# Up's first four blocks: four products in turn for all, weight sums made in DRAM, and the output factors in another pool

## The chip, the cores and the metric

The kernel runs on one core of a Trainium2 chip. The metric is device time in microseconds (us) of one execution. Three runs of the kernel before are shown, and one further execution was profiled.

The engines go by the profile's names: PE multiplies matrices (PEld is its weight load), DVE works elementwise, ACT applies functions and copies, POOL here fills memory and issues transfers, SP issues transfers. An engine takes its instructions in one fixed order.

## The reference

One decoder block on 512 rows of 2048 channels, in float32:

```
z = rms_norm(x, norm1_g) @ w_in                       # input projection
o_rw, o_att = rwkv7_mix(z...), swa_attention(z...)    # two mixers
x = x + (g_rw * (o_rw @ w_branch[:RW]) + g_att * (o_att @ w_branch[RW:])) @ w_out
u = rms_norm(x, norm2_g) @ w_up                       # 2048 -> 2 * 5632, "Up"
c = causal_conv3(u) ; val, gate = split(c, 2)
x = x + (silu(gate) * val) @ w_down                   # "Down"
```

## The kernel before

**Stages.** Input projection with both mixers; branch products; output product (`w_out`); Up with convolution and gate; Down. Every float32 operand of a large product is split into a high part (ACT, a copy to the rounded format `F32R`) and a low part (DVE, the difference), and a product is three matmuls: high-high, high-low, low-high.

**Products of halves.** Output product, Up and Down cut both operands into 2 x 2 halves and run seven products of halves in place of eight, with sums and differences of the halves (Strassen's scheme in Winograd's form).

For the output product and Down, the sums of weights are made in DRAM while the input projection runs. `jobs` (L216) lists them, 120 in all: 32 for `o`, 88 for `dn`. `sums_along` (L224) takes the next: SP copies a piece of 512 KB in DRAM, POOL adds a second piece by an accumulating transfer. `load_w` (L233), the loader of the projection's and the branch stage's weights, calls it at every third load (`wp["step"]`, L167), later at every fourth and twelfth; Up calls it for the jobs left (L1194).

**Up.** 44 blocks `f`, each a `Block` (L1043): 128 channels of `val` and `gate`, contracted over two halves of 1024, for two halves of the 512 rows. The left factors of the seven products are weights, the right factors (`bq`) are made once from the normalised rows:

| product | weights | right factor | sums into |
|---|---|---|---|
| P1 | a11 = w[0,0] | b11 | X |
| P2 | a12 = w[0,1] | b21 | Z |
| P7 | s3 = w[0,0] + w[1,0] | t3 | Y |
| P6 | a11 + s1 | t2 | X |
| P5 | s1 = w[1,0] + w[1,1] | t1 | X |
| Q4 | a22 = w[1,1] | t4 | Y |
| P3 | a11 + s1 + a12 | b22 | X |

`load` (L1050) lets SP fetch a tile of 512 KB; for s3 and s1, POOL then adds the second weight by an accumulating transfer. `sums` (L1058) makes the left factors of P6 and P3 on DVE (L1063). `parts` (L1065) splits a left factor: ACT makes `whi` (L1069), DVE `wlo` (L1070), in three buffers each. `mm` (L1073) issues 24 matmuls (L1087). `out` (L1090) copies X to `u` on ACT (L1103) and adds Y or Z on DVE (L1105, L1107). X and Z of blocks 0 to 3 share one PSUM bank. `u` has two buffers, for even and odd blocks. `conv` (L1109) is the convolution and gate of a block in five parts, seven for odd blocks.

**Order.** `pin` (L203) is `keep_in_program_order`: pinned instructions of an engine keep the order of the program. What isn't pinned is placed by the framework's planner, by priority and readiness.

`steps` (L1140) lists the products: for blocks 0 to 3 (`NPRE`) P1 four times, P2 four times, P7 four times, then the other four products in pairs of blocks; from block 4 on, block by block. `run(i)` (L1186) first splits the weights of step i + 2 (`prep`, L1174), then issues the matmuls and outputs of step i. `prep` also issues the next loads and takes one part of a convolution, two in a stretch. Loads go into a ring of six tiles `raw` and one of two tiles `a11`, and a load waits until the tile's earlier user is done. Of blocks 0 to 3, w[0,0] and w[0,1] are loaded twice (`p11`, `p12`, then `a11`, `a12`).

**From output product to Up.** In the last of the output product's seven rounds (L1205 to L1224), `normalise` scales the first half of the rows, `transposed` (L1009) turns q11 and q21 by PE, and `split_q` (L1032) splits them to b11 and b21, 2048 elements a row. `taken_out` (L957) adds the last round's product to x (L968), and `row_done` squares it. The second half of the rows is scaled by the transposing matmul itself, with `diagonals` (L1001) as its right side. The calls from L1237 to L1279 interleave the first twelve steps with the transposes of q12 and q22 and with the differences and splits of the other five right factors. These, in the version before, are not pinned.

**Output factors.** `fetch` (L929) loads a pair of the output product's right factors from DRAM into the pool `hp` (L864): three buffers on the right side of memory, opened ahead of the branch stage.

Of the kernel before, what the change touches and what calls it, by code (L numbers as in the profile page):

```python
# [134 lines left out]
def block_kernel(ctx: ExitStack, tc: tile.TileContext, d: Dims, a: dict, out: bass.AP):  # L135
# [79 lines left out]

    jobs = []  # L216
    for w in ("o", "dn"):
        for kinds in (
            (("s1", (1, 0), (1, 1)), ("s3", (0, 0), (1, 0))),
            (("s2", "s1", (0, 0)),),  # L220
            (("s4", "s2", (0, 1)),),
        ):
            jobs += [(w, k, c, q) for c in range(NB[w]) for q in range(2) for k in kinds]
    def sums_along():  # L224

        if not jobs:
            return lambda: None
        w, (n, first, second), c, q = jobs.pop(0)
        dst = sum_d[w][n][c][q]
        pin(sync.dma_start(dst, quarter(w, first, c)[q], max_dma_last_dim=4096))  # L230
        return lambda: pool.dma_start(dst, quarter(w, second, c)[q], accum_op=ALU.add, max_dma_last_dim=4096)

    def load_w(src):  # L233
        nk, ncol = src.shape[1:]
        n = nk * ncol
        raw = wp["raw"].tile([P, 512], F32, name="raw", tag="raw")[:, :n].rearrange("p (k c) -> p k c", c=ncol)
        wp["last"] = sync.dma_start(raw, src)
# [3 lines left out]
        dve.tensor_tensor(lo, raw, hi.bitcast(F32), op=ALU.subtract)  # L241
        wp["n"] += 1
        if wp["n"] % wp["step"] == 0:
            sums_along()()
        return hi, lo
# [763 lines left out]
    def transposed(tps, i, q, dg=None):  # L1009
# [11 lines left out]
        for k in range(KH):  # L1021
            src, g = pss[k // 2][:, k % 2], col("n2g", i * KH + k)
            dst = q[:, 2 * k // KH, k % (KH // 2) * TH : (k % (KH // 2) + 1) * TH]
            if k % 2:
                dve.tensor_scalar(dst, src, g, None, op0=ALU.mult)
            else:
                act.activation(dst, src, AF.Copy, scale=g)

    def halves(t):
        return t.rearrange("p (a k) s -> p a (k s)", a=2)  # L1030

    def split_q(n, q):  # L1032
        hi, lo = (halves(x) for x in bq[n])
        act.activation(hi, q, AF.Copy)
        dve.tensor_tensor(lo, q, hi.bitcast(F32), op=ALU.subtract)

    us = []
    dve.tensor_scalar(cw[:, 0:3, NF:], cw[:, 0:3, NF:], -1.0, None, op0=ALU.mult)


    NPRE = 4

    class Block:  # L1043
# [3 lines left out]
        def __init__(self, f):  # L1047
            self.f, self.w, self.hl = f, {}, {}

        def load(self, n):  # L1050
            f, w = self.f, self.w
            at = {"p11": (0, 0), "p12": (0, 1), "a11": (0, 0), "a12": (0, 1), "s3": (0, 0), "s1": (1, 0), "a22": (1, 1)}
            w[n] = raw_tile("a11", 2) if n in ("a11", "p11") else raw_tile()
            sync.dma_start(w[n], a["w_up"][(f, *at[n])])
            if n in ("s3", "s1"):
                pool.dma_start(w[n], a["w_up"][f, 1, int(n == "s1")], accum_op=ALU.add)

        def sums(self, n):  # L1058

            w = self.w  # L1060
            if n in ("P6", "P3"):
                t = w["a11"]
                pin(dve.tensor_tensor(t, t, w["s1" if n == "P6" else "a12"], op=ALU.add))  # L1063

        def parts(self, n):  # L1065
            one = "ap"[self.f < NPRE]
            t = self.w[{"P1": one + "11", "P2": one + "12", "P7": "s3", "P6": "a11", "P5": "s1", "Q4": "a22", "P3": "a11"}[n]]
            hi, lo = (hlp.tile([P, WC], F32R, name=f"w{e}", tag=f"w{e}") for e in ("hi", "lo"))
# [4 lines left out]
        def mm(self, n):  # L1073
# [4 lines left out]
            if n == "P7":  # L1078
                self.Y = upy.tile([P, S], F32, name="Y", tag="Y")[:, :TH]
            ps = getattr(self, {"P2": "Z", "P7": "Y", "Q4": "Y"}.get(n, "X"))  # L1080
            start = n in ("P1", "P7") or n == "P2" and self.f >= NPRE
            whi, wlo = (x.rearrange("p (k c) -> p k c", c=P) for x in self.hl.pop(n))
# [7 lines left out]
        def out(self, n):  # L1090
# [3 lines left out]
            if n == "P1" and self.f < NPRE:  # L1094
                self.t1 = up.tile([P, TH], F32, name="t1", tag="t1", bufs=NPRE)
                pin(act.activation(self.t1, X, AF.Copy))
                return

            i, j, ps, first = {"P1": (0, 0, X, True), "P2": (0, 0, Z, False), "P6": (1, 0, X, True), "P5": (1, 1, X, True),
                               "Q4": (1, 0, Y, False), "P3": (0, 1, X, True)}[n]  # L1100
# [5 lines left out]
            else:  # L1106
                pin(dve.tensor_tensor(u, self.t1 if n == "P2" and self.f < NPRE else u, ps, op=ALU.add))  # L1107

# [40 lines left out]
    queue, order = [], {x: i for i, x in enumerate(steps)}  # L1149
    loads = [(f + e, n) for f in range(0, NPRE, 2) for n in ("p11", "p12") for e in range(2)] + [(f, "s3") for f in pre]  # L1150
    for f in range(NF):
        loads += [(f, n) for n in ("a11", "s3", "s1", "a12", "a22") if n != "s3" or f >= NPRE]
    held = {True: [], False: []}
    for f, n in loads:
        kind = n in ("p11", "a11")
        users = {"p11": ("P1",), "p12": ("P2",), "s3": ("P7",), "s1": ("P5", "P6"), "a22": ("Q4",)}.get(n, ("P3",))
        ring, deep = held[kind], 2 if kind else 6
# [28 lines left out]
    def run(i):  # L1186
        f, n = steps[i]
        prep(i + 2, 2 if 3 * NPRE <= i < 7 * NPRE else 1)
        B[f].mm(n)
        if n != "P2" or f >= NPRE:  # L1190
            B[f].out(n)
        if n == "P3":
# [8 lines left out]
    with tc.tile_pool(name="sqp", bufs=1, side="right", reuse_waits="tile") as sqp:  # L1201
# [3 lines left out]
        for i in range(len(PRODUCTS)):  # L1205
# [6 lines left out]
            for c in range(NB["o"]):  # L1212
                steps_of("o", i, acc[nm], c, hp)
                if last and c == NB["o"] - 4:
                    transposed(tps, 0, q11)
                    split_q("b11", q11)
                if last and c == NB["o"] - 3:
                    transposed(tps, 1, q21)
                    split_q("b21", q21)
            if last:  # L1220
# [24 lines left out]
    tpx.close()  # L1245
    run(4)
    dve.tensor_tensor(q12, q22, q12, op=ALU.subtract)
    split_q("t3", q12)
    tcx.close()
    x1q.close()  # L1250
    run(5)
    run(6)
    split_q("t1", q11)
    run(7)
    upy = psx.enter_context(tc.tile_pool(name="uppy", bufs=4, space=PSUM, side="right", reuse_waits="tile"))
    run(8)
    dve.scalar_tensor_tensor(q11, q11, -1.0, q22, op0=ALU.mult, op1=ALU.subtract)
    split_q("t2", q11)
    run(9)
    run(10)  # L1260
    split_q("b22", q22)
    run(11)
    dve.scalar_tensor_tensor(q21, q11, -1.0, q21, op0=ALU.mult, op1=ALU.subtract)
    split_q("t4", q21)
    x1s.close()
    upu = upx.enter_context(tc.tile_pool(name="upu", bufs=1, side="left", reuse_waits="tile"))
    for i in range(2):
        u = upu.tile([P, 2, S + 2], F32, name=f"u{i}")
        pool.memset(u[:, :, 0:2], 0.0)
        us.append(u)  # L1270
    upcx = ExitStack()
    upc = upcx.enter_context(tc.tile_pool(name="upc", bufs=1, side="right", reuse_waits="tile"))
    hp0 = upcx.enter_context(tc.tile_pool(name="hhl0", bufs=1, side="right", reuse_waits="tile"))
    for f in range(2):
        B[f].out("P2")
    for i in range(3 * NPRE, len(steps)):
        run(i)
        if steps[i] in ((2, "P6"), (2, "Q4")):
            B[2 + (steps[i][1] == "Q4")].out("P2")  # L1279
        if steps[i] == (NF - 2, "P7"):  # L1280
# [105 lines left out]
```

## Time and profile before

| | us |
|---|---|
| median of 3 runs | 2830.01 (2829.44 to 2835.7) |
| the profiled execution | 2830.7 |
| its span in the profile | 2828.9 |
| PE busy | 2774.4 |
| DVE busy | 1987.5 |
| ACT busy | 1342.1 |
| POOL busy | 225.1 |

The granted clock of the profiled execution is 0.996 on average. An engine's busy time is the union of its instructions; matmuls overlap each other, so a matmul lasts longer in the profile than the distance from one to the next. A row of the waits gives who waited for whom, the total in us, how often, and the longest. A row of the chain gives start, length and what ran; "x24" is the number of instructions merged. A row of the groups gives line, engine and operation, output and inputs with their shape, count, then busy time and mean ns of one, then the idle time ahead of them. In the profile's names, X stands for the bank of X and Z, `x` for the rows of x and the halves q, `b` and `t` for right factors, `raw` and `a` for weight tiles, `c` for the tiles of the convolution, and `dg` for the diagonals.

### The profile page before, as it was taken

What the parts mean: (1) busy time and instruction counts of PE and PEld (TensorE: products, weight loads), DVE (VectorE), ACT (ScalarE), POOL (GpSimd) and SP (SyncE); (2) the same over time, 40 slices, a digit from 0 to 9 for tenths busy, and PEclk for the clock granted to TensorE, in tenths of its full rate; (3) what the DMA queues carried; (4) which work ended last, traced back from release to release, by engine and by line L of the source; (5) the groups of instructions that cost most, each with busy time, mean ns of one, the idle gap of its engine ahead of it and who ended that gap; (6) DMA issues with size and microseconds to landing.
All of it is one profiled execution on the core that took longest, in us unless ns stands there. A gap on an engine that the chain in (4) does not pass through costs nothing.

```text
span 2828.9 us, 45923 instructions
## 1 busy us (share of the span) xinstructions
PE 2774.4 (98%) x17450; PEld 2403.0 (85%) x17450; DVE 1987.5 (70%) x3437; ACT 1342.1 (47%) x2256; POOL 225.1 (8%) x299
## 2 busy tenths in 40 slices
PE   7999999999999999999999899999999999999999
PEld 5777777777777777888888899999999999888887
DVE  4588677777777774545678777878787878655555
ACT  4355445444544553322465455555545555444444
POOL 0001000000000001011010011011101110000000
PEclk9999999999999999999999999999999999999999
DMA  7865766666666667878777789888988897877775
GB/s 216 227 159 163 187 167 168 175 164 158 175 162 171 160 165 223 234 248 292 237 251 211 210 235 241 229 229 227 241 236 222 228 242 228 315 245 241 256 256 190
DMA packets 223726, 607.04 MB, mean 215 GB/s; under 512 B 24448, under 2 KB 44560, under 8 KB 222480
## 3 DMA queue, kind: packets, MB, share of 16 engines
q1 hardware_dynamic: 156096, 432.64, 47.1%
q0 software_dynamic: 36064, 132.14, 24.5%
q10 hardware_dynamic: 31344, 39.31, 4.0%
q8 instruction: 137, 2.24, 0.3%
q14 instruction: 85, 0.70, 0.1%
HBM read 554.38 MB, written 174.40 MB: 258 GB/s over the span
## 4 chain that ended last, share of the span: by engine, by line
PE 87%; DVE 5%; ACT 3%; DMA 2%; issue 1%; SPq 0%; POOL 0%; ACTq 0%; DVEq 0%; POOLq 0%
PE X L1087 18%; PE X L954 11%; PE acc L256 9%; PE acc L255 9%; PE acc L257 9%; PE Y L954 9%; PE Y L1087 9%; PE Z L1087 4%; DVE wlo L241 1%; PE psS L740 1%; PE psG L731 1%; PE bulk L623 1%; PE bulk L673 1%; PE bulk L534 1%; ACT whi L240 1%
## 5 line engine op out<-in xcount | busy, mean ns | idle before, releaser
L255 PE MATMUL acc<-xhi,whi 128*128 128x512 f32 x1152 | 462.9, 402 | 1.9 <-DVE xlo L301 1.9
L257 PE MATMUL acc<-xhi,wlo 128*128 128x512 f32 x1152 | 463.8, 403 | 0.0
L256 PE MATMUL acc<-xlo,whi 128*128 128x512 f32 x1152 | 462.2, 401 | 0.0
L947 DVE TENSOR_TENSOR wlo<-raw,whi 128x1024 fp32r<-128x1024 f32 x210 | 256.9, 1224 | 205.1 <-ACT whi L946 204.9
L240 ACT ACTIVATE whi<-raw 128x512 fp32r<-128x512 f32 x352 | 220.0, 630 | 375.7 <-PE acc L256 295.1
L946 ACT ACTIVATE whi<-raw 128x1024 fp32r<-128x1024 f32 x210 | 222.8, 1061 | 290.6 <-PE X L954 152.9
L241 DVE TENSOR_TENSOR wlo<-raw,whi 128x512 fp32r<-128x512 f32 x352 | 241.3, 689 | 167.1 <-ACT whi L240 146.9
L1087 PE MATMUL X<-b,whi 128*128 128x256 f32 x1472 | 270.2, 284 | 2.3 <-DVE u L1107 0.9
L1087 PE MATMUL X<-t,whi 128*128 128x256 f32 x1408 | 259.6, 285 | 10.3 <-DVE u L1107 9.8
L1070 DVE TENSOR_TENSOR wlo<-raw,whi 128x1024 fp32r<-128x1024 f32 x176 | 215.0, 1222 | 77.6 <-ACT whi L1069 77.3
L1087 PE MATMUL Y<-t,whi 128*128 128x256 f32 x1408 | 257.1, 283 | 0.0
L255 PEld LDWEIGHTS acc<-xhi,whi 128*128 128x128 f32 x1152 | 217.6, 189 | 43.4 <-issue 2.5
L256 PEld LDWEIGHTS acc<-xlo,whi 128*128 128x128 f32 x1152 | 217.5, 189 | 41.9 <-issue 3.3
L257 PEld LDWEIGHTS acc<-xhi,wlo 128*128 128x128 f32 x1152 | 217.5, 189 | 38.3 <-issue 1.1
L1069 ACT ACTIVATE whi<-a 128x1024 fp32r<-128x1024 f32 x132 | 139.3, 1056 | 216.5 <-DVE a L1063 214.3
L1087 PEld LDWEIGHTS X<-b,whi 128*128 128x128 f32 x1472 | 230.7, 193 | 3.1 <-issue 2.4
L1087 PEld LDWEIGHTS X<-t,whi 128*128 128x128 f32 x1408 | 221.6, 194 | 10.9 <-DVE u L1107 7.2
L1087 PEld LDWEIGHTS Y<-t,whi 128*128 128x128 f32 x1408 | 219.8, 192 | 0.0
L1087 PE MATMUL X<-b,wlo 128*128 128x256 f32 x736 | 209.3, 284 | 2.1 <-DVE wlo L1070 2.1
L1070 DVE TENSOR_TENSOR wlo<-a,whi 128x1024 fp32r<-128x1024 f32 x132 | 161.7, 1226 | 67.3 <-ACT whi L1069 66.7
L1087 PE MATMUL X<-t,wlo 128*128 128x256 f32 x704 | 200.4, 285 | 0.0
L1087 PE MATMUL Y<-t,wlo 128*128 128x256 f32 x704 | 199.4, 283 | 0.0
(339 smaller groups left out, 5762.1 us busy)
## 6 DMA issues: line engine op xcount, KB each, us to landing
raw<-in_w_up_dram SPq DMA_DIRECT2D x180, 512.0 KB, 4.6
raw<-in_w_z_dram SPq DMA_DIRECT2D x288, 256.0 KB, 3.9
s_dn<-in_w_dn_dram POOLq DMA_DIRECT2D x88, 512.0 KB, 5.9
raw<-in_w_up_dram POOLq DMA_DIRECT2D x88, 512.0 KB, 8.7
raw<-s_dn SPq DMA_DIRECT2D x88, 512.0 KB, 3.8
raw<-in_w_dn_dram SPq DMA_DIRECT2D x66, 512.0 KB, 3.5
a<-in_w_up_dram SPq DMA_DIRECT2D x48, 512.0 KB, 6.9
s_dn<-in_w_dn_dram SPq DMA_DIRECT2D x44, 512.0 KB, 4.9
```

Source lines behind the costliest of these rows:

```text
L240: act.activation(hi, raw, AF.Copy)
L241: dve.tensor_tensor(lo, raw, hi.bitcast(F32), op=ALU.subtract)
L255: pe.matmul(acc, whi[:, j], xhi[:, k], start=first, stop=False)
L256: pe.matmul(acc, whi[:, j], xlo[:, k], start=False, stop=False)
L257: pe.matmul(acc, wlo[:, j], xhi[:, k], start=False, stop=last)
L534: pe.matmul(ps, w[:, i], ads[:, i], start=i == lo, stop=i == hi - 1)
L946: act.activation(whi, wr, AF.Copy)
L947: dve.tensor_tensor(wlo, wr, whi.bitcast(F32), op=ALU.subtract)
L954: pe.matmul(dst, l[:, q, ts], r[:, es], start=fst and j == 0, stop=lst and j == 2, skip_group_check=True)
L1069: pin(act.activation(hi, t, AF.Copy))
L1070: pin(dve.tensor_tensor(lo, t, hi.bitcast(F32), op=ALU.subtract))
L1087: pin(pe.matmul(ps, l[:, k], r[:, k], start=start and k + i == 0, stop=last and i == 2, skip_group_check=True))
```

## The change

The four left factors s3, s1, P6 and P3 of blocks 0 to 3 are made in DRAM, by 16 jobs put between those of `o` and of `dn`; P6 accumulates s1, and P3 starts as a copy of P6. `load_w` calls `sums_along` once more in every fifteen loads of the input projection. For these blocks `load` then fetches each of the seven left factors once, in the order of the steps, and `sums` does nothing.

The steps run P1, P2, P7 and P6 for all four blocks, then P5, P3 and Q4: interleaved for blocks 0 and 1, one after the other for block 2, then for block 3. The outputs of blocks 2 and 3 come later (`apart`): P5 and P3 sum into Z, and `out` adds Z on DVE. Every block of the four adds P2's Z to P1's copy `t1` on DVE and copies the result to `u` with a copy on ACT (`place`).

`split_q` becomes `high` (ACT) and `low` (DVE). From b21's lower half on they are pinned, as are the differences of the halves and the evacuation of the second pair of transposes, and the first 19 steps are written out with each `prep` in its place. The stretch in which `prep` takes two parts of a convolution ends four steps later.

Of the output factors, the first round's pairs 0 and 1 use a pool of two buffers on the right (`hp0`), all others a pool of three on the left (`hp`), opened after the branch stage in its memory.

```diff
+    NPRE = 4
+    up_d = {(f, n): dram.tile([P, DH], F32, name=f"{n}_u{f}") for f in range(NPRE) for n in ("s3", "s1", "P6", "P3")}
...
+    def up_jobs():
+        for f in range(NPRE):
+            w, t = a["w_up"][f], {n: up_d[f, n] for n in ("s3", "s1", "P6", "P3")}
+            jobs.extend(((t["s3"], w[0, 0], w[1, 0]), (t["s1"], w[1, 0], w[1, 1]), (t["P6"], w[0, 0], t["s1"]),
+                         (t["P3"], t["P6"], w[0, 1])))
...
+        if w == "o":
+            up_jobs()
...
-        if wp["n"] % wp["step"] == 0:
+        if wp["n"] % wp["step"] == 0 or wp["step"] == 3 and wp["n"] % 15 == 10:
             sums_along()()
...
-    hp = hps.enter_context(tc.tile_pool(name="hhlC", bufs=3, side="right", reuse_waits="tile"))
+    hp0 = hps.enter_context(tc.tile_pool(name="hhlC", bufs=2, side="right", reuse_waits="tile"))
...
+    hp = hps.enter_context(tc.tile_pool(name="hhlO", bufs=3, reuse_waits="tile"))
...
+            put = pin if dg else free
...
-    def split_q(n, q):
+    def high(n, q, pin=pin):
+        pin(act.activation(halves(bq[n][0]), q, AF.Copy))
+
+    def low(n, q, pin=pin):
         hi, lo = (halves(x) for x in bq[n])
-        act.activation(hi, q, AF.Copy)
-        dve.tensor_tensor(lo, q, hi.bitcast(F32), op=ALU.subtract)
+        pin(dve.tensor_tensor(lo, q, hi.bitcast(F32), op=ALU.subtract))
...
+            self.apart = 2 <= f < NPRE
...
-            sync.dma_start(w[n], a["w_up"][(f, *at[n])])
-            if n in ("s3", "s1"):
+            sync.dma_start(w[n], up_d[f, n] if (f, n) in up_d else a["w_up"][(f, *at[n])])
+            if n in ("s3", "s1") and f >= NPRE:
...
-            if n in ("P6", "P3"):
+            if n in ("P6", "P3") and self.f >= NPRE:
...
+            ps = getattr(self, "Z" if self.apart and n in ("P5", "P3") else into)
+            start = n in ("P1", "P7") or n == "P2" and self.f >= NPRE or n == "P5" and self.apart
...
+            if self.f < NPRE:
+                if n == "P2":
+                    pin(dve.tensor_tensor(self.t1, self.t1, Z, op=ALU.add))
+                    return
+                if self.apart and n != "P1":
+                    if n != "P6":
+                        i, j, more = {"P5": (1, 1, (Z, Y)), "P3": (0, 1, (Z,)), "Q4": (1, 0, (Y,))}[n]
+                        u = us[self.f % 2][:, i, 2 + j * TH : 2 + (j + 1) * TH]
+                        pin(act.activation(u, X, AF.Copy))
+                        for ps in more:
+                            pin(dve.tensor_tensor(u, u, ps, op=ALU.add))
+                    return
...
+        def place(self):
+            pin(act.activation(us[self.f % 2][:, 0, 2 : 2 + TH], self.t1, AF.Copy))
...
-    steps = [(f, n) for n in ("P1", "P2", "P7") for f in pre]
-    for f in range(0, NPRE, 2):
-        steps += [(f + e, n) for e, n in ((0, "P6"), (0, "P5"), (1, "P6"), (0, "P3"), (1, "P5"), (0, "Q4"), (1, "P3"), (1, "Q4"))]
+    steps = [(f, n) for n in ("P1", "P2", "P7", "P6") for f in pre]
+    steps += [(f, n) for f, n in ((0, "P5"), (1, "P5"), (0, "P3"), (0, "Q4"), (1, "P3"), (1, "Q4"))]
+    steps += [(f, n) for f in pre[2:] for n in ("P5", "P3", "Q4")]
...
+    OWN = ("a11", "P6")
+    loads = [(f, {"P1": "a11", "P2": "a12", "P7": "s3", "P5": "s1", "Q4": "a22"}.get(n, n)) for f, n in steps if f < NPRE]
...
-        prep(i + 2, 2 if 3 * NPRE <= i < 7 * NPRE else 1)
+        if i > 4 * NPRE + 2:
+            prep(i + 2, 2 if i < 8 * NPRE else 1)
         B[f].mm(n)
...
+        if f < NPRE and (n == "P6" if f < 2 else n == "P5"):
+            B[f].place()
...
-                steps_of("o", i, acc[nm], c, hp)
+                steps_of("o", i, acc[nm], c, hp0 if i == 0 and c < 2 else hp)
...
+    prep(2)
+    dg = diagonals(1)
     run(0)
-    dg = diagonals(1)
+    low("b21", q21)
+    prep(3)
     run(1)
+    prep(4)
+    transposed(tps, 0, q12, dg)
     run(2)
-    transposed(tps, 0, q12, dg)
-    run(3)
-    dve.tensor_tensor(q11, q11, q12, op=ALU.subtract)
+    prep(5)
+    pin(dve.tensor_tensor(q11, q11, q12, op=ALU.subtract))
     transposed(tps, 1, q22, dg)
     tpx.close()
+    run(3)
...
+    run(7)
+    upy = psx.enter_context(tc.tile_pool(name="uppy", bufs=4, space=PSUM, side="right", reuse_waits="tile"))
+    low("t1", q11)
+    prep(10)
+    pin(dve.scalar_tensor_tensor(q11, q11, -1.0, q22, op0=ALU.mult, op1=ALU.subtract))
+    run(8)
...
+    run(10)
+    prep(13)
+    low("t2", q11)
...
+    prep(18)
+    high("t4", q21)
+    run(16)
+    prep(19)
+    low("t4", q21)
```

More of the change, by code (lines that the diff above doesn't have):

```diff
@@ L222, in block_kernel @@
         ):
-            jobs += [(w, k, c, q) for c in range(NB[w]) for q in range(2) for k in kinds]
+            jobs += [(sum_d[w][n][c][q], *(quarter(w, x, c)[q] for x in (first, second)))
+                     for c in range(NB[w]) for q in range(2) for n, first, second in kinds]
+        if w == "o":
+            up_jobs()
     def sums_along():
@@ L227, in sums_along @@
             return lambda: None
[L228 to L231, printed above, removed]
+        dst, first, second = jobs.pop(0)
+        pin(sync.dma_start(dst, first, max_dma_last_dim=4096))
+        return lambda: pool.dma_start(dst, second, accum_op=ALU.add, max_dma_last_dim=4096)
     def load_w(src):
@@ L1106, in out @@
             else:
[L1107 removed]
+                pin(dve.tensor_tensor(u, u, ps, op=ALU.add))
+        def place(self):
+            pin(act.activation(us[self.f % 2][:, 0, 2 : 2 + TH], self.t1, AF.Copy))
         def conv(self, part):
@@ L1270, in block_kernel @@
         us.append(u)
+    prep(14)
+    run(12)
+    prep(15)
+    high("b22", q22)
+    run(13)
+    prep(16)
+    low("b22", q22)
+    run(14)
+    prep(17)
+    pin(dve.scalar_tensor_tensor(q21, q11, -1.0, q21, op0=ALU.mult, op1=ALU.subtract))
+    run(15)
+    prep(18)
[3 more added lines that the diff above has]
+    low("t4", q21)
+    x1s.close()
     upcx = ExitStack()
@@ L1273, in block_kernel @@
     hp0 = upcx.enter_context(tc.tile_pool(name="hhl0", bufs=1, side="right", reuse_waits="tile"))
-    for f in range(2):
-        B[f].out("P2")
-    for i in range(3 * NPRE, len(steps)):
+    run(17)
+    prep(20)
+    run(18)
+    for i in range(4 * NPRE + 3, len(steps)):
         run(i)
-        if steps[i] in ((2, "P6"), (2, "Q4")):
-            B[2 + (steps[i][1] == "Q4")].out("P2")
         if steps[i] == (NF - 2, "P7"):
```

63 lines of the change are left out of this document (29 added, 34 removed).

## The prediction

> **What bounds the kernel now.** I read the page first, then the waits of PE, then the chain of waits around the start of Up.
>
> ```profile
> span 2828.9 us, 45923 instructions
> PE 2774.4 (98%) x17450; PEld 2403.0 (85%) x17450; DVE 1987.5 (70%) x3437; ACT 1342.1 (47%) x2256; POOL 225.1 (8%) x299
> ```
>
> PE is busy for all but 54.5 us of the span, and no matmul is added or removed. So the change can only win idle or slow-clock time of PE, and only where its order is new. PE's waits over the whole span, as total, times, longest:
>
> ```profile
> PE X L1087 <- DVE u L1107: 10.7, 3, 7.0
> ...
> PE X L1087 <- DVE wlo L1070: 2.1, 1, 2.1
> ...
> PE X L1087 <- DVE x L968: 0.9, 1, 0.9
> ```
>
> L1087 is Up's matmul, and these waits all lie at Up's start. The chain of waits (start, length, what) gives their frame:
>
> ```profile
> 1490.52 8.86 PE X L1087 x72
> 1499.38 3.57 PE ps_t L1018 x32
> 1505.82 3.36 PE ps_t L1018 x30
> ...
> 1557.16 11.61 DMA raw<-in_w_up_dram
> 1573.50 14.05 PE X L1087 x96
> ...
> 1605.98 2.88 PE Z L1087 x24
> 1608.86 5.76 PE X L1087 x48
> ```
>
> An undisturbed product (24 matmuls) takes 2.88 us. From 1490.52 to the start of block 5's P1 at 1608.86 + 2.88 = 1611.74 lie 121.22 us. In them PE runs 33 products, 95.04 us, and two sets of transposes, 6.93 us. **Lost now: 121.22 - 101.97 = 19.25 us.** After that the products follow each other at 2.88 us, so this stretch is all there is to win. Part of the loss is clock; in these windows the columns are length, busy time and count of PE, PEld, DVE, ACT and POOL, the granted clock, DMA share and GB/s:
>
> ```profile
> 1519.00:1520.00 1.00, 0.00 (x0) 0.00 (x0) 1.00 (x2) 1.00 (x2) 0.17 (x1) 1.00 1.08 160
> 1520.00:1521.00 1.00, 0.00 (x0) 0.00 (x0) 1.00 (x2) 1.00 (x2) 0.15 (x2) 0.84 0.65 82
> ...
> 1522.00:1524.00 2.00, 2.00 (x11) 2.00 (x11) 2.00 (x3) 0.12 (x1) 0.00 (x0) 0.50 0.99 266
> ...
> 1537.00:1539.00 2.00, 0.00 (x0) 0.00 (x0) 2.00 (x1) 0.00 (x0) 0.00 (x0) 1.00 0.74 229
> ...
> 1569.00:1578.00 9.00, 4.50 (x21) 4.50 (x22) 6.76 (x8) 4.31 (x6) 0.86 (x1) 0.50 0.57 128
> ```
>
> After a gap of about 2 us near 1519 the clock fell to 0.50 for some 3.4 us, which costs half of that, 1.7 us; the gap at 1537, as long, cost nothing; the 7.0 us wait brought a spell of about 5 us of slow work, 2.5 us lost.
>
> **What makes the gaps.** DVE works in a fixed order and is the engine in arrears:
>
> ```profile
> 1485.21 2.29 DVE L1035 TENSOR_TENSOR b<-x,b 128x2048 fp32r<-128x2048 f32 x1 [0.85 <-ACT b L1034]
> 1487.42 2.35 DVE L1070 TENSOR_TENSOR wlo<-a,whi 128x1024 fp32r<-128x1024 f32 x2
> 1489.69 2.48 DVE L968 SCALAR_TENSOR_TENSOR x<-X,x 128x512 f32<-128x512 f32 x4
> 1493.11 0.16 DVE L988 TENSOR_REDUCE ss<-ssp 128x2 f32<-128x8 f32 x1 [0.94 <-ACT sqc L983]
> ...
> 1496.70 0.48 DVE L1006 TENSOR_SCALAR dg<-ident,rq 128x128 f32<-128x128 f32 x2
> ...
> 1568.79 1.22 DVE L1063 TENSOR_TENSOR a<-a,raw 128x1024 f32<-128x1024 f32 x1 [1.45 <-DMA raw<-in_w_up_dram]
> ```
>
> The 7.0 us wait ends with L1107, which stood behind the sum L1063, which stood behind an accumulating transfer that took 11.61 us. The other waits come from whole-half operations (2.29 us) let in ahead of weight splits. The prices, as busy time, mean ns and idle before:
>
> ```profile
> L1070 DVE TENSOR_TENSOR wlo<-raw,whi 128x1024 fp32r<-128x1024 f32 x20 | 24.3, 1221 | 5.9 <-ACT whi L1069 5.7 <-PE Y L1087 0.2
> ...
> L1124 DVE SCALAR_TENSOR_TENSOR c<-u,par,c 128x512 f32<-128x512 f32 x16 | 11.9, 747 | 3.9 <-ACT c L1121 3.9
> L1063 DVE TENSOR_TENSOR a<-a,raw 128x1024 f32<-128x1024 f32 x9 | 11.0, 1218 | 1.4 <-DMA raw<-in_w_up_dram 1.4
> L1035 DVE TENSOR_TENSOR t<-x,t 128x2048 fp32r<-128x2048 f32 x4 | 9.2, 2288 | 1.2 <-ACT t L1034 1.2
> ...
> L1107 DVE TENSOR_TENSOR u<-u,Y 128x256 f32<-128x256 f32 x4 | 1.7, 417 | 0.5 <-PE Y L1087 0.5
> ```
>
> ```profile
> L1069 ACT ACTIVATE whi<-raw 128x1024 fp32r<-128x1024 f32 x20 | 20.8, 1049 | 5.7 <-PE X L1087 3.1 <-PE Y L1087 2.5
> ...
> L1034 ACT ACTIVATE t<-x 128x2048 fp32r<-128x2048 f32 x4 | 7.6, 1908 | 1.6 <-DVE x L1247 1.4
> ...
> L1103 ACT ACTIVATE u<-X 128x256 f32<-128x256 f32 x15 | 5.7, 378 | 11.6 <-PE X L1087 11.6
> ```
>
> **Up's start, part by part.** Removed: eight sums on DVE (8 x 1.22 = 9.8 us) and eight accumulating transfers on POOL; the 28 loads on SP stay 28. Added: four adds on DVE (4 x 0.42 = 1.7 us, the Z of blocks 2 and 3) and four copies on ACT (4 x 0.38 = 1.5 us, `place`). With this the causes of all 19.25 us are gone. What the new order puts in their place, each as a wait of PE:
>
> - Start. b21's lower half (2.29 us) leaves the queue ahead of L968, whose first piece releases PE: at most the 0.9 us wait is won; I take a **gain of 0.8**.
> - a. The transposes of q12 now come after the second P1, not the third. PE gets there 5.76 us after about 1489.7, at 1495.5. Their diagonals took 1493.11 to 1497.18 with one split between; starting 0.8 earlier they end at 1496.4, and at 1498.6 if b21's lower half slips in. PE's order of transposes is not pinned, so it may take P1 first and wait for nothing. **1.0** (0 to 3.1).
> - b. Three buffers hold split weights, so the split for step 13 waits for PE to end step 10: ACT 1.05 + DVE 1.22, and in DVE's pinned order t2's lower half, 2.29, stands behind it, 4.56 in all. PE has only step 11 (2.88) before it needs t2. **1.9** with handovers (0 if DVE runs ahead, to 2.5).
> - c. In the same way t4's lower half stands behind the split of step 19. ACT holds t4's upper half (1.91), an output copy (0.38) and that split (1.05) in a row, then DVE 1.22 + 2.29: 6.85 against two products, 5.76. **1.2** (0 to 2).
> - d. Block 2 runs P5 and at once P3, both into Z; P3 may not start before P5's output has added Z. With nothing queued that is 0.38 + 0.42 and handovers, 1.0. But DVE's order has, from the end of block 0's Q4, ahead of that add: two output adds, six parts of convolutions (0.75 each, 0.66 back to back) and three splits, some 8.1 us, and about 3.8 us in which it waits for ACT's share of those parts. 11.9 against three products, 8.64. **3.3** (1.0 to 3.5).
> - e. Block 3 the same, with one product more for DVE to catch up: **2.1** (1.0 to 2.5).
> - f. Block 4's first products meet the convolutions of 2 and 3, still in arrears, and an accumulating load again: **1.7** (0 to 3).
> - g. Clock: three of these gaps are of the size that cost 1.7 us once and nothing once. One spell, **1.7** (0 to 5.1).
>
> Waits a to g sum to 12.9 us.
>
> The clock row has its rule in the Trainium skill, "TensorE: Matmul & The Clock Gate", section "What's actually happening": half clock after an idle window of about 3.4 us. By it no gap here would slow PE for sure, term g would be 0 and the sum 2822.3. The trace does not agree: its clock fell at a gap of about 2 us, so g stays.
>
> **The input projection.** The 16 sums become 16 copies on SP and 16 accumulates on POOL, in the job list after those of `o`; all later jobs move back, and 17 more calls (every fifteenth load) make room. 120 jobs become 136; 103 instead of 86 are issued before the branch stage. Transfer time and queue:
>
> ```profile
> s_o<-in_w_o_dram POOLq DMA_DIRECT2D x32, 512.0 KB, 6.3
> ...
> s_o<-s_o SPq DMA_DIRECT2D x16, 512.0 KB, 5.2
> ...
> hraw<-h_o SPq DMA_DIRECT2D x28, 256.0 KB, 3.9
> ```
>
> ```profile
> 50.00:100.00 50.00, 50.00 (x232) 40.43 (x232) 21.05 (x61) 14.12 (x23) 4.67 (x6) 1.00 0.87 227
> 200.00:1100.00 900.00, 888.61 (x5599) 703.34 (x5598) 666.31 (x1618) 429.31 (x967) 76.53 (x106) 1.00 0.67 168
> 1100.00:1300.00 200.00, 199.31 (x876) 163.59 (x875) 96.96 (x170) 59.10 (x101) 25.76 (x37) 1.00 0.83 254
> ```
>
> If all transfers were jobs, 0.67 would become 0.67 x 103 / 86 = 0.80. At 0.83 and at 0.87 PE is busy all but 0.7 us of 250. What hides the jobs is the loads' lead (four raw tiles and four split ones); without it each job could cost a piece of a load. **0.5** (0 to 5, about 0.3 for each of 17).
>
> A rule against the change stands in the Trainium skill, "DMA: Bandwidth & Descriptors", section "Issuing engines are not separate DMA queues": transfers of all issuers share 16 engines, so POOL's accumulates compete with SP's loads. Taken alone it would put the term at its upper end, 5, and the sum at 2828.5; by the rows the share has room, and the term stays 0.5.
>
> **Output factors.** Two pairs stay on the right; from the third on they lie where the branch stage's tiles were, so that fetch waits on SP for the end of the branch matmuls.
>
> ```profile
> 1329.22 22.39 PE X L954 x96
> ```
>
> A quarter of this product is 5.6 us, so the third pair is needed 11.2 us after the stage's start; fetch 3.9 and splits of about 1.3 us fit. **0**; without the cover about 5 once.
>
> **Sum.** The profiled run took 2830.7 us, the median shown is 2830.0. Gain 19.25 + 0.8, less 12.9, less 0.5 = 6.65: **2824.0**, 6.0 under the median. About 0.2%, 5.7 us, is what a measurement of this kernel can tell from no change.
>
> **Rivals.**
>
> - DVE and ACT are not in arrears: d and e at 1.0, c, f and g at 0, a and b as above. 5.4 in all with the projection: gain 14.6, **2816**. For it: 9.8 us less DVE work. Against: PE's products set a pace of 2.88 us, and a step of blocks 0 to 3 has about 1.2 + 1.4 + 0.5 us of DVE work. Chance 0.2.
> - The waits move, and their sum stays: a to f at their upper ends (16.6), three clock spells (5.1), 0.5: 22.2 against 20.05, **2833**. For it: the pinned orders leave an engine no way round a late operand. Chance 0.2.
> - Slower: P3's copy reads what P6's accumulate writes, so SP, with the raw loads behind, holds until it has landed: 5.2 + 6.3 = 11.5 us after P6's copy, while three loads take PE 36 x 50/232 = 7.8. Four holds of 3.7, 14.8 us on top of the forecast: **2839**. It decides once the loads' lead is under 3.7 us. Against it, in 200 to 1100 us SP's own waits are mostly for free buffers, so it runs ahead:
>
> ```profile
> SPq L237 <- DVE wlo L241: 498.1, 147, 14.0
> ```
>
> Chance 0.1.
>
> **How the numbers follow.** The forecast has 0.5, over 2819 to 2829. The range 2815 to 2833 takes in the first two rivals and leaves out the third and the tails. Faster by over 0.2% (under 2824.3): half of the forecast, 0.27, and the first rival, 0.2: 0.47. Same: the rest of the forecast and most of the second rival, 0.39. Slower: the third rival and the tail of the second, 0.14.
>
> **What would show it.** Right: no sum L1063 and no accumulating load before block 4; block 5's P1 some 12 to 14 us after 33 x 2.88 + 6.93 us of work; PE waits for t2's and t4's lower half and for the adds of Z in blocks 2 and 3. Wrong: a wait of PE for a raw load or a weight split in the projection, PE idle at the start of the output stage, or Up's first products without gaps.

## The result, and the profile after

| | before | after |
|---|---|---|
| median of 17 runs each, us | 2829.55 (2827.45 to 2835.7) | 2837.53 (2832.17 to 2843.51) |
| ratio to before, 95% interval | | 1.0024 (1.0016 to 1.0032) |
| span of the profiled execution, us | 2828.9 | 2840.8 |

The kernel became slower by 0.24%, where 0.2% faster was forecast. The profiled execution of the changed kernel is one of its longer ones, so the stages are compared in it, and the verdicts on causes rest on the runs below.

Four stretches make up the 11.9 us between the two spans. The output product starts at 1349.67 instead of 1329.22: **20.45 us lost ahead of it.** From there to Up's first product it takes 156.55 us instead of 161.30: **4.75 won.** Up's start, to block 5's P1, takes 115.01 us instead of 121.22: **6.21 won.** The rest takes 2.4 us more. 20.45 - 4.75 - 6.21 + 2.4 = 11.9.

**The input projection** lost the most. Windows of the changed kernel, columns as in the prediction (length, busy time and count of PE, PEld, DVE, ACT, POOL, granted clock, DMA share, GB/s):

```profile
200.00:1100.00 900.00, 876.45 (x5487) 691.55 (x5486) 655.62 (x1587) 423.22 (x953) 87.08 (x119) 0.99 0.72 180
...
220.00:230.00 10.00, 7.03 (x25) 5.19 (x26) 7.45 (x17) 1.93 (x4) 0.00 (x0) 0.66 0.15 47
400.00:410.00 10.00, 7.33 (x35) 5.88 (x34) 6.21 (x15) 0.85 (x2) 1.50 (x2) 0.83 0.69 152
410.00:420.00 10.00, 10.00 (x47) 8.08 (x47) 6.77 (x15) 2.18 (x5) 0.00 (x0) 0.83 0.49 125
900.00:910.00 10.00, 7.83 (x32) 6.05 (x31) 6.20 (x15) 1.07 (x3) 0.80 (x1) 0.83 0.52 134
```

PE is idle 23.55 us of the 900, where it was 11.39 before (900 - 888.61): 12.2 us more. The four short windows show the clock down to 0.66 and 0.83, 1.00 in the same windows before: 10 x (0.34 + 0.17 + 0.17 + 0.17) = 8.5 us. Together 20.7, against a loss of 20.45; a little of the slow clock falls into the idle time and counts twice. The DMA share rose from 0.67 to 0.72, far from the 0.83 at which PE was busy. What PE waited for in 200 to 1340 us (total, times, longest):

```profile
PE bulk L686 <- DVE XIW L213: 5.4, 14, 0.6
PE psS L753 <- DVE UV L749: 5.0, 5, 2.2
PE mi L468 <- DVE plo L213: 3.3, 1, 3.3
PE psG L744 <- DVE SV L757: 2.7, 1, 2.7
```

The first was there before, the other three are new. No wait for a weight load or split is among them: the mixers' own products wait for DVE. The chain of waits at 396 us shows what held DVE (rows under 0.3 us are left out):

```profile
396.40 3.01 DMA rsd<-rsT
399.47 0.48 SPq L351
400.00 5.32 DMA rsb<-rsd
...
405.77 0.69 DVE kk L565
406.78 0.30 DVE SV L757
407.21 1.09 PE psG L744 x4
```

This is `head_rows` (L329 before, L342 after): the row factors of the head norm, 4 KB, go to DRAM as `rsd` and come back, spread over partitions, as `rsb`. DVE multiplies them into `kk` (and `qn` in the attention). While it waits for `rsb`, the state updates of the other pair of heads (`SV`, `UV`) stand behind it, and PE behind those. The group of `rsb`, after:

```profile
  DMA rsb<-rsd: 18.0, 9
who waited for it (us, times):
  DVE kk L565: 13.7, 7
  DVE qn L369: 4.3, 2
```

and before:

```profile
  DMA rsb<-rsd: 5.2, 2
```

DVE sat idle 18.0 us in nine waits for it instead of 5.2 in two.

**The output product.** Two of its seven rounds, after; before each took 22.4:

```profile
1349.67 22.20 PE X L967 x96
1371.87 21.76 PE Y L967 x96
```

The round whose first half still uses the old place has 22.20, the later ones 21.76, for the same 96 matmuls.

**Up's start.** First its first matmul in the timeline, then the chain's rows at the other end of the stretch:

```profile
1506.22 0.40 PE L1102 MATMUL X<-b,whi 128*128 128x256 f32 x2
```

```profile
1618.35 5.76 PE X L1102 x48
```

Block 5's P1 starts at 1618.35 + 2.88 = 1621.23. 115.01 - 101.97 of undisturbed work: **13.0 us lost, where the prediction had 12.9.** The waits of PE in it, and the clock after the longest of them:

```profile
PE X L1102 <- DVE u L1124: 4.2, 2, 3.2
PE X L1102 <- DVE t L1052: 1.8, 1, 1.8
PE Y L1102 <- DVE t L1052: 0.8, 1, 0.8
PE Z L1102 <- DVE wlo L1084: 0.8, 1, 0.8
PE ps_t L1032 <- DVE dg L1020: 0.8, 1, 0.8
PE X L1102 <- ACT u L1130: 0.7, 1, 0.7
```

```profile
1586.00:1591.00 5.00, 3.93 (x20) 3.93 (x21) 3.32 (x7) 2.28 (x3) 0.00 (x0) 0.66 0.98 252
```

### The profile page after: what moved, and what is told of

Read it like the earlier page. It is cut to its first block, busy times and chain, and to the rows that moved or that the text cites. A ratio compares the mean times of both kernels' runs of the same rounds, so it can differ in the third digit from the quotient of the medians.

```text
span 2840.8 us, 45932 instructions
## 1 busy us (share of the span) xinstructions
PE 2779.1 (98%) x17450; PEld 2408.6 (85%) x17450; DVE 1980.7 (70%) x3433; ACT 1343.1 (47%) x2260; POOL 232.0 (8%) x307
## 4 chain that ended last, share of the span: by engine, by line
PE 85%; DVE 6%; ACT 3%; DMA 2%; issue 2%; SPq 0%; ACTq 0%; DVEq 0%
PE X L1102 17%; PE X L967 11%; PE acc L269 9%; PE acc L268 9%; PE acc L270 9%; PE Y L967 9%; PE Y L1102 8%; PE Z L1102 4%; DVE wlo L254 1%; DMA rsb<-rsd 1%; PE psS L753 1%; PE psG L744 1%; PE bulk L636 1%; PE bulk L686 1%; ACT whi L253 1%
## 5 line engine op out<-in xcount | busy, mean ns | idle before, releaser
L959 ACT ACTIVATE whi<-raw 128x1024 fp32r<-128x1024 f32 x210 | 222.5, 1060 | 286.1 <-PE X L967 141.2
L1083 ACT ACTIVATE whi<-raw 128x1024 fp32r<-128x1024 f32 x180 | 188.7, 1049 | 24.1 <-ACT whi L1083 15.6
```

The costliest lines, as they stand in the source:

```text
L959: act.activation(whi, wr, AF.Copy)
L1083: pin(act.activation(hi, t, AF.Copy))
```

## The experiments

Theory: the added sums make the row factors late, DVE blocks, PE follows. Rivals: the changed program is planned differently everywhere; the sums cost bandwidth wherever they stand; SP stands still where P3's copy waits for P6's accumulate (the prediction's third rival). "Start" is the first matmul of the output product in the profiled execution. Each ratio is to runs of the kernel before on the same chip.

| kernel | median us | ratio, 95% interval | start us |
|---|---|---|---|
| before | 2829.55 | | 1329 |
| after | 2837.53 | 1.0024 (1.0016 to 1.0032) | 1350 |
| e1_plain | 2820.97 | 0.9971 (0.9962 to 0.9980) | 1329 |
| e2_sums | 2843.34 | 1.0056 (1.0043 to 1.0068) | 1342 |
| e3_pool | 2826.89 | 0.9996 (0.9987 to 1.0004) | 1327 |
| e4_actrows | 2852.47 | 1.0085 (1.0071 to 1.0098) | 1360 |
| e5_noextra | 2821.68 | 0.9971 (0.9960 to 0.9982) | 1330 |
| e6_kinds | 2832.11 | 1.0008 (0.9999 to 1.0016) | 1341 |
| e7_phase | 2841.81 | 1.0044 (1.0032 to 1.0057) | 1355 |
| e8_noextra_kinds | 2821.07 | 0.9968 (0.9955 to 0.9981) | 1329 |
| e10_phase2 | 2826.90 | 0.9985 (0.9977 to 0.9994) | 1330 |
| e11_turn | 2819.41 | 0.9970 (0.9958 to 0.9982) | 1328 |
| e12_align | 2831.17 | 1.0003 (0.9994 to 1.0012) | 1329 |
| e13_middle | 2827.23 | 0.9989 (0.9979 to 0.9998) | 1328 |

### Are the sums the cause?

e1_plain takes them, and the added calls, out of the changed kernel: blocks 0 to 3 load plain quarters of `w_up` in place of the sums. e2_sums puts the sums and the added calls into the kernel before, where nothing reads them. The edit of e1_plain:

```diff
-        if w == "o":
-            up_jobs()
...
-        if wp["n"] % wp["step"] == 0 or wp["step"] == 3 and wp["n"] % 15 == 10:
+        if wp["n"] % wp["step"] == 0:
...
-            sync.dma_start(w[n], up_d[f, n] if (f, n) in up_d else a["w_up"][(f, *at[n])])
+            sync.dma_start(w[n], a["w_up"][(f, *at[n])])
```

> The changed kernel without the sixteen sums in DRAM and without the seventeen added calls in the input projection; blocks 0 to 3 load plain quarters of w_up in their place, so these blocks' part of the output is not the reference's. Row theory (the head norm's small transfers come late behind the sums' copies, VectorE blocks on them, TensorE follows): the input projection is as before, the first L534/L547-type milestone and the output product start within 2 us of the kernel before, and the whole comes to 2829.5 - 6.4 (Up's start) - 4.6 (shorter output products) = 2818.5 us. Rival (the projection was lengthened by a changed order of the whole program, not by the sums): the output product still starts 13 to 20 us late and the time stays at 2835 to 2838.

> The kernel before with the sixteen sums added to its list of jobs and the seventeen added calls, nothing else; no one reads the sums. Row theory: the projection takes 20 us longer, 2850 us, with VectorE's waits for rsb near 18 us as in the changed kernel. Rival (changed order of the program): as before, 2830 us.

Without the sums the projection is back where it was and the whole beats the kernel before by 0.29%; the sums alone cost the kernel before 0.56%, 13 us of it ahead of the output product. The planner's order elsewhere is not the cause. 20 us were expected of e2_sums and 14 came; DVE's waits for `rsb` were 13.7 us there, not 18.

### Is it SP's queue, or the transfers themselves?

```diff
-            sync.dma_start(rd, sm)
+            act.dma_start(rd, sm)
...
-                sync.dma_start(rb[h * HD : (h + 1) * HD], src[h : h + 1].to_broadcast([HD, S]))
+                act.dma_start(rb[h * HD : (h + 1) * HD], src[h : h + 1].to_broadcast([HD, S]))
```

> The changed kernel with the head norm's row factors (rsd out, rsb in, twice) issued on ScalarE's DMA queue, where no copy of a sum stands ahead of them. Row theory: rsb lands about 3.3 us after its issue again, VectorE's waits for rsb fall from 18 us to near 5 us, and of the 20 us lost in the projection some 10 to 15 come back: 2823 to 2828 us (a part could go to ScalarE's own order, since a transfer there waits behind its activations). Rival (the loss comes from the bandwidth that the sums take from all loads, or from their number): the waits move little, 2836 to 2839 us.

A miss: 15 us slower than the changed kernel. Who waited for the group of `rsd`, issued by ACT's queue (us, times):

```profile
  ACT whi L253: 14.3, 3
  ACT UV L748: 9.4, 3
  DVE kk L565: 7.4, 6
  DVE qn L369: 2.4, 1
```

DVE's waits for `rsb` did fall, from 18.0 to 9.8 us (7.4 and 2.4). But ACT issues `rsb` only once `rsd` has landed, and in that time its own work, the weights' splits `whi` above all, stands still. Nor did a queue without the copies of the sums make the trip quick: from `rsd` to `rsb` it took 2.3 to 7.6 us in the eight pairs of heads, 3.3 in the median, where on SP's queue the median was 4.0 in the changed kernel and 2.2 in the kernel before. So the copies ahead in SP's queue alone do not explain the slow trip. The Trainium skill, "DMA: Bandwidth & Descriptors", section "Issuing engines are not separate DMA queues", has a rule that agrees: all issuers share the same transfer engines, so another issuer saves only the time to issue.

### Number, hold or moment?

Four kernels tell these apart. e5_noextra drops the added calls, and Up takes the sums left over, two at each pair of blocks. e6_kinds keeps them but orders the sums so that none waits for the one just ahead. e8_noextra_kinds does both. e7_phase has sixteen added calls for the seventeen and puts them at fixed places of the period of a pair of heads (24 loads).

In e5_noextra:

```diff
-        if wp["n"] % wp["step"] == 0 or wp["step"] == 3 and wp["n"] % 15 == 10:
+        if wp["n"] % wp["step"] == 0:
...
-                wp["add"] = sums_along()
+                wp["add"] = sums_along(), sums_along()
             else:
-                wp["add"]()
+                for add in wp["add"]:
+                    add()
```

In e6_kinds, where the three lists hold s3 and s1, then P6, then P3:

```diff
...
+        jobs.extend(ups[0] + ups[1] + ups[2])
```

In e7_phase:

```diff
+    EXTRA = [n for n in range(80, 236) if n % 24 in (1, 17)] + [94, 118, 142]
...
-        if wp["n"] % wp["step"] == 0 or wp["step"] == 3 and wp["n"] % 15 == 10:
+        if wp["n"] % wp["step"] == 0 or wp["step"] == 3 and wp["n"] in EXTRA:
```

> The changed kernel without the added calls in the projection, so that every sum falls at the same loads as in the kernel before; the sixteen jobs left over are taken in Up, two at each pair of blocks instead of one. Timing theory (what costs is that an added sum's 512 KB are in flight when the head norm's 4 KB row goes out, so the row lands after 4.5 to 6.5 us instead of 3, and VectorE, which had 1 us to spare, blocks): only the four sums that are held for another's landing disturb, the output product starts within 5 us of 1329, the time is 2819 to 2824 us. Hold theory (SP stands still at the copy of P3 until P6 has landed, and everything behind it is late): half of the loss stays, 2828 to 2831 us. Density theory (each of the sixteen sums costs its us wherever it stands): Up loses what the projection gains, 2835 to 2838 us.

> The changed kernel with the sixteen sums in another order: all eight s3 and s1 first, then the four P6, then the four P3, so that none waits for the one just before it; the added calls stay. Timing theory: the added calls still drift through the period of a pair, 2832 to 2838 us. Hold theory: the loss of the projection goes, 2820 to 2824 us. Density theory: 2835 to 2838 us.

> The changed kernel with the same number of added calls (16), but each at a fixed place in the period of a pair, in its gates and its r tile, away from the head norm's rows, instead of at every fifteenth load. Order of the sums as in the change. Timing theory: VectorE uses rsb 6.9 us after rsT is made in nearly all pairs, as before, the output product starts within 6 us of 1329, 2819 to 2825 us. Hold theory: the four holds stay, 2828 to 2831 us. Density theory: 2835 to 2838 us.

> No added calls, as in the second kernel of this call's first line, and the sums ordered by kind: neither drift nor holds. Timing theory and hold theory: the projection as before, 2818 to 2822 us, the least of the four. Density theory (in Up now): 2830 us or more.

e5 has the same sixteen sums, at the old moments and with the tail of the list in Up, and loses nothing against e1_plain: neither the sixteen sums nor the longer tail in Up costs anything that shows. It also has seventeen sums fewer ahead of the output product, 98 for 115, so it does not tell the number from the moments. e8 takes the holds away too and gains nothing more.

The holds are there. SP's waits at the copies of P3's sums, in 200 to 1340 us of the changed kernel (total, times, longest):

```profile
SPq L243 <- DMA P_u<-s_u: 12.7, 4, 7.0
```

e5 has two, 4.7 us in all, and e6 none. e6 is about 5 us better than the changed kernel, but its sums also fall at other moments (DVE's waits for `rsb` are 11.6 us instead of 18.0), so what the holds alone cost is not shown. e7, expected at 2819 to 2825, came out worst of the four. Its timeline shows why (start, length; POOL's row starts a sum's accumulate, 512 KB; other loads and copies are left out):

```profile
896.85 0.81 POOL L245 DMA_DIRECT2D s_dn<-in_w_dn_dram  x1 [9.31 <-DMA s_dn<-in_w_dn_dram]
898.27 0.29 SPq L348 DMA_DIRECT2D rsd<-rsT  x1
903.60 1.12 SPq L352 DMA_DIRECT2D rsb<-rsd  x2
907.61 0.69 DVE L566 TENSOR_TENSOR kk<-kk,rsb 128x512 f32<-128x512 f32 x1 [2.41 <-DMA rsb<-rsd]
```

The place chosen was wrong: load 1 of the period is issued 18 us before the row factors, and the sum after it then had 8.4 us from its copy to its accumulate instead of 4.9 in e5, so that the accumulate started 1.4 us ahead of `rsd`. SP then waited 5.3 us for 4 KB. The kernel before, with its fixed rhythm, did not meet this at any pair after the first:

```profile
872.36 0.80 POOL L231 DMA_DIRECT2D s_dn<-in_w_dn_dram  x1 [10.79 <-DMA s_dn<-in_w_dn_dram]
877.09 0.29 SPq L334 DMA_DIRECT2D rsd<-rsT  x1
879.03 1.12 SPq L338 DMA_DIRECT2D rsb<-rsd  x2
883.93 0.68 DVE L552 TENSOR_TENSOR kk<-kk,rsb 128x512 f32<-128x512 f32 x1
```

There the second of the two loads of `rsb` was issued at 879.56 and, by the semaphore records of the trace, had landed by 882.53: **1.4 us ahead of DVE's need.** In the seven pairs after the first this margin was 0.1 to 1.8 us. The changed kernel, at the same pair:

```profile
892.93 0.81 POOL L244 DMA_DIRECT2D s_dn<-in_w_dn_dram  x1 [2.63 <-DMA s_dn<-in_w_dn_dram]
893.76 0.29 SPq L347 DMA_DIRECT2D rsd<-rsT  x1
899.38 1.12 SPq L351 DMA_DIRECT2D rsb<-rsd  x2
903.03 0.69 DVE L565 TENSOR_TENSOR kk<-kk,rsb 128x512 f32<-128x512 f32 x1 [2.34 <-DMA rsb<-rsd]
```

So e10_phase2, with seventeen added calls, one more than e7, moves the calls at places 1 and 22 of the period to places 8 and 13, loads that are issued after the row factors; those at place 17 stay:

```diff
...
+    EXTRA = [n for n in range(80, 236) if n % 24 in (8, 17)] + [85, 109, 133]
```

> As the kernel with added calls at fixed places, the same sixteen in number, but other places: at the loads that SP issues some 5 to 15 us after the head norm's rows (gate and k tile), not in the 20 us ahead of them. Timing theory (a sum's second transfer that starts within 2 us before the row's 4 KB store holds that store): the row's store lands in 2.5 to 3 us again, VectorE uses rsb 6.9 us after rsT in nearly all pairs, 2820 to 2827 us. Density theory (the same number of sums in the projection costs the same wherever they stand): 2835 to 2842 us as with the other places.

```profile
873.80 0.81 POOL L245 DMA_DIRECT2D s_dn<-in_w_dn_dram  x1 [10.62 <-DMA s_dn<-in_w_dn_dram]
878.38 0.29 SPq L348 DMA_DIRECT2D rsd<-rsT  x1
881.67 1.12 SPq L352 DMA_DIRECT2D rsb<-rsd  x2
885.34 0.69 DVE L566 TENSOR_TENSOR kk<-kk,rsb 128x512 f32<-128x512 f32 x1
```

With one sum more, it is 14.9 us less between the two medians. The accumulate now starts 4.6 us ahead and `kk` waits for nothing. DVE still waited at four of the eight pairs of heads; in three of these the accumulate had crept to 1.9 to 2.9 us ahead of `rsd`.

In eight kernels (before, after, e2, e5, e6, e7, e8, e10) seven pairs of heads each give 56 such readings (the first pair, late in all of them, is left out), from the start of the last accumulate to `rsd`, and from `rsd` to `rsb`:

| accumulate started ahead of `rsd` by | readings | `rsd` to `rsb`: least, median, most |
|---|---|---|
| 0.6 to 2.7 us | 16 | 3.4, 4.5, 7.0 us |
| 4.1 to 5.1 us | 30 | 1.5, 2.2, 3.9 us |

Of the other ten, five lie between the two rows of the table (2.4 to 5.4 us). Four have 5.6 us or more and yet 3.1 to 4.7; there the next accumulate came within 3.7 us. One, in the changed kernel, has 0.3 and only 1.3; there the load was the late one: `rsb` was issued at 599.03, and DVE, after 1.2 us of waiting, began `kk` at 605.81.

So the moment decides most of it: ahead of the output product e7 lost 26 us and e10, with one sum more, 1. That the number costs nothing is not shown. e10's median lies 5.2 us above e5's, the intervals of the two ratios overlap only just, and its profiled run, the one that starts the output product at 1330, is 4 us under its median.

### What the output factors' place does

e3_pool is the kernel before with the change's pools and nothing else; e12_align moves its old place by 32 bytes; e13_middle puts the factors between the two places.

```diff
-    hp = hps.enter_context(tc.tile_pool(name="hhlC", bufs=3, side="right", reuse_waits="tile"))
+    hp0 = hps.enter_context(tc.tile_pool(name="hhlC", bufs=2, side="right", reuse_waits="tile"))
...
+    hp = hps.enter_context(tc.tile_pool(name="hhlO", bufs=3, reuse_waits="tile"))
...
-                steps_of("o", i, acc[nm], c, hp)
+                steps_of("o", i, acc[nm], c, hp0 if i == 0 and c < 2 else hp)
```

In e12_align:

```diff
+    tcp.tile([P, 8], F32, name="room")
```

In e13_middle, on top of e3_pool:

```diff
+    hps.enter_context(tc.tile_pool(name="room", bufs=1, side="right")).tile([P, 7848], F32, name="room")
-    hp = hps.enter_context(tc.tile_pool(name="hhlO", bufs=3, reuse_waits="tile"))
+    hp = hps.enter_context(tc.tile_pool(name="hhlO", bufs=3, side="right", reuse_waits="tile"))
```

> The kernel before with only the pool of the output factors changed, as in the change. Place theory (TensorE's matmuls of the output product are shorter with the stationary factors in the lower pool): 96 matmuls take 21.76 us instead of 22.4, the time is 2829.5 - 4.6 = 2825 us. Rival (the output product's gain in the changed kernel comes from fewer transfers beside it, not from the pool): 22.4 us for 96, 2829.5 us.

> The kernel before with a tile of 32 bytes a partition put ahead of the output factors in the same pool, so that they start at a multiple of 64 bytes (176768) instead of 32 beyond one (176800); nothing else. Alignment theory: 96 matmuls of the output product take 21.76 us as in the lower pool, 2826 us. Region theory (the upper part of the memory is slower for them): 22.4 us, 2829.5 us.

> The kernel before with the output factors of all products but the first two steps in a pool that starts at byte 133120 of a partition, between the place of the changed kernel (109056) and that of the kernel before (176800), with room left empty above it. If the pitch changes at one border below 133120: 22.3 to 22.4 us for 96 matmuls and 2829.5 us as before; if the border lies above 151552 or the distance does not matter and only the place of the kernel before is bad: 21.76 us and 2826 us.

A round of 96 matmuls in the chain of e3_pool:

```profile
1371.40 21.76 PE X L954 x96
```

and of e12_align:

```profile
1351.41 22.31 PE Y L955 x96
```

In e13_middle the timeline gives the pitch, ten matmuls in 2.27 us, 21.8 us for 96:

```profile
1399.65 0.39 PE L954 MATMUL Y<-whi,hlo 128*128 128x512 f32 x1
...
1401.92 0.39 PE L954 MATMUL Y<-wlo,hhi 128*128 128x512 f32 x1
```

The pool alone shortens the rounds, with the same transfers beside them. In the times it is worth 2 to 4 us at the most: e3's interval contains no change, e13's just doesn't. The start at a multiple of 64 bytes hardly matters (22.31), and a border below 133120 is ruled out. Whether the upper addresses as such are slower, or their distance to the other operand matters, stays open.

### Can the waits for Z be taken out?

e11_turn is e8 with blocks 2 and 3 in turn.

```diff
-    steps += [(f, n) for f in pre[2:] for n in ("P5", "P3", "Q4")]
+    steps += [(f, n) for f, n in ((2, "P5"), (3, "P5"), (2, "P3"), (2, "Q4"), (3, "P3"), (3, "Q4"))]
...
-            prep(i + 2, 2 if i < 8 * NPRE else 1)
+            prep(i + 2, 3 if i in (22, 23) else 2 if i < 8 * NPRE else 1)
```

> The kernel without added calls and with the sums by kind, and blocks 2 and 3 in turn (P5 of both, then P3 and Q4 of each) with one more convolution step of the blocks before at the two steps ahead, so that P3 no longer follows its own block's P5 and need not wait for VectorE's add of Z. If the two waits for u (4.2 us) are lost time of TensorE: 2821 - 3 to 4 = 2817 us. Rival (VectorE is the bound there and the wait comes back at the next product): 2821 us.

```profile
PE X L1105 <- DVE u L1127: 2.5, 1, 2.5
...
PE X L1105 <- ACT u L1133: 1.4, 1, 1.4
```

The wait for `u` on DVE fell from 4.2 to 2.5 us and 1.4 came back at a product that waits for ACT. From Up's first product to block 5 the two kernels take the same time within 0.1 us, and their ratios agree: the rival held, the products there wait for DVE's and ACT's arrears, in whatever order they come.

**A version that beats both:** e5 or e8, the change without the added calls and with two sums at each pair of Up's blocks: 0.29% and 0.32% under the kernel before. e11 adds nothing that can be told from e8.

## Why the prediction was wrong

- **Up's start: right.** Its terms, forecast and measured: a 1.0 and 0.8; b 1.9 and 1.8; c 1.2 and 0.8; d 3.3 and 3.2; e 2.1 and 1.0 (4.2 - 3.2); f 1.7 and 1.7 (0.8 and 0.7 above, and 0.2 for a split). g, one spell at half clock, 1.7: after d's wait the clock in 1586 to 1591 us was 0.66, and 5 x 0.34 is 1.7. The start gain of 0.8 came as well: no wait for L981, the old L968, is left. The terms sum to 11.0 of the 13.0 lost; 0.45 of the rest are longer transposes (3.81 and 3.57 us in the chain), and the cause of the others stays open. So the waits and their places were right, and that the total fell within 0.1 us was in part luck. In term d the prices shown (2 x 0.42, 6 x 0.66, 3 x 1.22) add up to 8.5 us of DVE work, not 8.1.
- **The input projection: the step that failed.** "0.5 (0 to 5, about 0.3 for each of 17)" priced the sums against what they could take from the weight loads: the DMA share has room and the loads have a lead. Both held, and no weight load came late. What it left out was a transfer with no lead at all, the row factors' trip through DRAM, whose group in the trace of before already showed two waits, 5.2 us, and at the pairs that did not wait 0.1 to 1.8 us to spare. The added sums delayed that trip, DVE stood still, and PE behind it, with spells of slow clock. In the profiled run the term is 20.45 us; in the runs, after against e5_noextra, 2837.53 - 2821.68 = 15.9. None of the signs that the prediction named for this stage, a wait for a raw load or a weight split, showed it.
- **The Trainium skill's rule** on issuing engines ("DMA: Bandwidth & Descriptors") was set aside because "by the rows the share has room". Its direction held: a transfer of one queue was delayed by one of another. A mean share says nothing of what two transfers at the same moment do to each other.
- **Output factors:** forecast 0 with a risk of 5 at the fetch. The fetch cost nothing, and the rounds became 4 us shorter for a reason that no row of the trace before showed.
- **The rivals.** The third, slower at 2839, had the place (SP and the projection in arrears) and nearly the price, and its four holds came, 12.7 us of SP's time where it had 14.8. But no matmul waited for a raw load, so its mechanism is not what cost the time, and the holds alone (e5 against e8) cost nothing that shows. The first rival, 2816, did not come true even without the added calls: e5 took 2821.68, nearer to the forecast's 2824.0, with d at its full size. Nor did the second: the waits of Up's start cost 13.0 us, not 21.7 (16.6 + 5.1).
- **The sum.** 2824.0 without the projection's 0.5, and with the 4 us won in the output product, is 2819.5; e5, without the loss, took 2821.68. With the 15.9 us between e5 and the changed kernel it is 2835.4, against 2837.53. 1.6 us of the rest are in the profiled run a clock spell at the change from Up to Down, behind a wait that grew from 1.4 to 2.0 us:

```profile
2400.00:2420.00 20.00, 17.99 (x127) 16.73 (x126) 16.94 (x23) 12.73 (x18) 2.12 (x4) 0.92 0.70 234
```

## What to carry to other kernels

Before adding background transfers, look for the small round trip through DRAM that an in-order engine waits for, and measure its margin; the mean DMA share does not show it. Where the margin is a microsecond or two, keep the background work at the same moments of the period, or put it right behind the round trip: by the places of the added sums alone, e7 and e10 lie 14.9 us apart. When a change has two parts, try the gain without the part that only makes room for it: here that was the better kernel.

## What the hardware showed that was not expected

- A store of 4 KB to DRAM, up to the issue of the load that waits for it, took 2.2 us in the median when the last accumulating transfer of 512 KB had started 4.1 to 5.1 us earlier on another queue, and 4.5 us when it had started 0.6 to 2.7 us earlier.
- The pitch of the same 128x512 matmuls was 0.2333 us (22.4 / 96) with the stationary operand from byte 176800 of a partition, 0.2324 from 176768, and 0.2267 from 133120 or 109056.
- In the changed kernel PE's clock fell after idle times of 3.2 us (Up) and 2.0 us (Up to Down), and not after 1.8 us in Up. The length of the idle time does not settle it: the same 1.8 us at Up's start brought a clock of 0.50 in e6 (1544 to 1546 us), while 2.8 us in the kernel before (up to 1539.6 us) and 3.2 us in e4 (up to 1598.3 us) brought none.
